# Products of 512 columns from both parts of the activation, in place of two of 256

## The chip, the cores and the metric

The kernel runs on one core of one Trainium2 chip. The metric is the device time of one execution in microseconds; before the change it was 1375.06 us, the median of 3 runs (1374.87 to 1375.58).

## The reference, cut to what matters

The program is a block of three layers over 256 rows of 1024 numbers: a convolution mixer with a dense feed-forward network, an attention mixer with 8 experts, and a third layer with attention, a memory and a second dense feed-forward network. The change touches the convolution's input projection and both dense networks:

```python
b_gate, c_gate, u = jnp.split(h @ w_in, 3, axis=-1)     # h is 256 x 1024, w_in 1024 x 3072
v = c_gate * u                                          # then a causal convolution of width 3
...
x = x + (b_gate * conv) @ w_out
...
h = rmsnorm(x, norm_ffn[i])
x = x + (jax.nn.silu(h @ w_gate) * (h @ w_up)) @ w_down # w_gate, w_up 1024 x 2816
```

Everything is float32.

## The kernel before, in words

Float32 products are made of three faster ones. Each operand is split into a high part (rounded by ScalarE, `split_to`, L219) and a low part (the rest, subtracted by VectorE, L220); `mm3` adds up high x high, low x high and high x low (L225 to L227), all into one PSUM bank.

Weights come in chunks of 128 x 2048 (1 MB), loaded by SP into four raw buffers, and are split in two pieces of 128 x 1024 into three pairs of buffers. A chunk's load therefore waits until the chunk four places earlier is split, and a split waits until the products of the chunk three places earlier are done. `Body.run` walks through a list of steps and writes each engine's instructions in that order; `f` in an order string means one piece of a coming chunk. Every engine executes its own list in order.

The steps that matter:

- In the convolution, `x00` to `x11` (`features`) each use one chunk with two tiles of 128 weight columns. The weights are the still operand, the activation, turned so that its 1024 features lie in 8 blocks of 128 rows and the 256 positions in columns, is the moving one. Each tile gives one feature block of 128 x 256, in half a bank. `g0` to `g7` (`gated`) combine three such blocks and split the result; `o0`, `o1` and `zp` multiply it with the output weights. `C` loads constants, `T` makes the rope tables (`rope_tables`), which only the attention layer reads.
- In a feed-forward stage the first 512 columns of gate and up are made by rows (`a`, `A`), and turned by eight transposes on TensorE (`T`, `rows_turn`), whose two banks have the tag t. `u04` to `u21` (`up`) are made like the convolution's features: the gate half in one half of a bank, the up half in the other. `o` multiplies with the down weights and keeps four banks of tag b as sums.

PSUM has eight banks; six have the tag b, two the tag t. A bank is written again when all that reads its old contents is done.

Of the kernel before, what the change touches and what calls it, by code (L numbers as in the profile page):

```python
# [12 lines left out]
F32R = mybir.dt.float32r  # L13
# [3 lines left out]
AF = mybir.ActivationFunctionType  # L17
# [4 lines left out]
P = 128  # L22
D = 1024
S = 256
NT = S // P
KD = D // P
# [5 lines left out]
NH = 8  # L32
# [25 lines left out]
PIECES = 2  # L58
AHEAD = 2, 2

TAGS = dict(x8=2, n4=4, g4=1, c6=2, e1=6, q=4, w2=11, mk=1, vm=1, sel=2, mx=2, kr=1, ssr=1)
BANKS = dict(b=6, t=2)

WARM = 26
CONV_HEAD = ("zs00 zs01 zn0 zs10 zt f1 zs11 zn1 w")
CONV_ORDER = ("x00 x01 f1 f2 T x02 f2 x03 f2 f2 f2 C x04 f2 x05 g0 x06 g1 f2 f1 g2 x07 f1 f2 f1 f1 x08 o0 g3 f1 f2 "
    "f1 f1 g4 f2 x09 g5 x10 x11 f2 f1 o1 g6 g7 f2 zp000 f2 zp010 zp100 zp110 f2 zp001 zp011 f1 zr00 zp101 "
    "zr01 zp111 zs00 zs01 zn0 f1 f1 f2 zt zr10 f1 f2 f2 zs10 f1 zr11 f1 f1 zs11 zn1 f1")
FFN_HEAD = ("f1 f2 a00 f2 f1 a10 f2 f1 w a20 f1 f2 a21 a01 a30 f2 a31 f2 a11 f1 f2 f2 f2 f1 f1 f2 A u04 f2 f2 f2 "
    "f1 T f2 u05 f1 f1 f1 o0 o1 f2 f2 f2 f2 o2 f1 f2 f2 u06 f1 f2 u07 f1 f2 f1 f2 f1")  # L70
# [35 lines left out]
class Parts:  # L106


    def __init__(self, pieces):
        self.pieces = pieces  # L110

    def __call__(self, k, s=slice(0, S)):
        for k0, n, h, l in self.pieces:
# [4 lines left out]
class Body:  # L118
# [103 lines left out]
    def mm3(self, ps, a, b, start, stop):  # L222

        mm = self.nc.tensor.matmul
        mm(ps, lhsT=a[0], rhs=b[0], start=start, stop=False)  # L225
        mm(ps, lhsT=a[1], rhs=b[0], start=False, stop=False)  # L226
        mm(ps, lhsT=a[0], rhs=b[1], start=False, stop=stop)  # L227


    def row(self, name, n, tag=None):  # L230
# [153 lines left out]
    def conv(self, norm, nxt):  # L384
        nc, t_ = self.nc, self.t
        cin = [self.chunk(t_["conv_in"][i]) for i in range(12)]
        cout = [self.chunk(t_["conv_out"][i]) for i in range(4)]
        feat, got, acc = {}, {}, {}

        def features(i):  # L390
            c = cin[i]
            b = self.bank("b" if i % 3 != 1 else "t")
            for h in range(2):
                o = feat[2 * i + h] = b[:, h * S:(h + 1) * S]
                for k in range(KD):
                    w = slice((h * KD + k) * P, (h * KD + k + 1) * P)
                    self.mm3(o, c[w], norm.xT(k), k == 0, k == KD - 1)

        def gated(j):
            oc, ou, ob = (feat.pop(3 * j + i) for i in range(3))  # L400
            cw = self.cols[:, 0:24].rearrange("p (j w) -> p j w", w=3)
            cs, v, y, z = (self.buf("e1", [P, n]) for n in (S, S + 2, S, S))
            nc.scalar.copy(cs, oc)
            nc.gpsimd.memset(v[:, :2], 0.0)
            nc.vector.tensor_mul(v[:, 2:], cs, ou)
            nc.vector.tensor_scalar(y, v[:, :S], cw[:, j, 0:1], None, op0=ALU.mult)
            for q in (1, 2):
                nc.vector.scalar_tensor_tensor(y, v[:, q:q + S], cw[:, j, q:q + 1], y, op0=ALU.mult, op1=ALU.add)
            nc.vector.tensor_mul(z, y, ob)
            got[j] = self.split(z)  # L410

        def out(d):
            for r in range(2):
                self.project(acc, cout[d], r, got.pop(2 * d + r), d == 0 and r == 0)

        closing = self.closing(acc, [(cout[j // 2], j % 2, lambda j=j: got[j]) for j in range(4, 8)], nxt, False)
        self.play(CONV_HEAD, self.entering(norm))
        self.play(CONV_ORDER, {
            "x": lambda i, j: (lambda: features(10 * i + j), cin[10 * i + j]), "g": lambda j: (lambda: gated(j),),
            "o": lambda d: (lambda: out(d), cout[d]), "C": lambda: (self.constants,), "T": lambda: (self.rope_tables,), **closing})  # L420


    def ffn(self, norm, gu0, gu, down, nxt, orders):

        nc = self.nc
        c0 = [self.chunk(gu0[i]) for i in range(4)]
        cu = [self.chunk(gu[i]) for i in range(NF - 4)]
        cd = [self.chunk(down[i]) for i in range(NF // 2)]
        acc, got, rows = {}, {}, {}

        def row_part(i, t):

            if i % 2 == 0:
                rows[i // 2, t] = self.bank()
            for kk in range(4):
                k = 4 * (i % 2) + kk
                self.mm3(rows[i // 2, t], norm.xT(k, slice(t * P, (t + 1) * P)), c0[i][kk * 512:(kk + 1) * 512],
                         k == 0, k == KD - 1)

        def rows_act():  # L440
            hs = []
            for t in range(NT):
                sg, h = self.buf("w2", [P, 512]), self.buf("w2", [P, 512])
                nc.scalar.activation(sg, rows[0, t], AF.Silu)
                nc.vector.tensor_mul(h, sg, rows[1, t])
                hs.append(h)
            rows["h"] = hs

        def rows_turn():
            th, tl = self.buf("n4", [P, 4, S], F32R), self.buf("n4", [P, 4, S], F32R)  # L450
            for t in range(NT):
                b = self.bank("t")
                for k in range(4):
                    nc.tensor.transpose(b[:, k * P:(k + 1) * P], rows["h"][t][:, k * P:(k + 1) * P], self.ident)
                ts = slice(t * P, (t + 1) * P)
                self.split_to(th[:, :, ts], tl[:, :, ts], b.rearrange("p (k m) -> p k m", m=P))
            for k in range(4):
                got[k] = th[:, k], tl[:, k]

        def up(j):  # L460
            b = self.bank()
            for i in range(2):
                for k in range(KD):
                    w = slice((i * KD + k) * P, (i * KD + k + 1) * P)
                    self.mm3(b[:, i * S:(i + 1) * S], cu[j - 4][w], norm.xT(k), k == 0, k == KD - 1)
            sg, h = self.buf("e1", [P, S]), self.buf("e1", [P, S])
            nc.scalar.activation(sg, b[:, :S], AF.Silu)  # L467
            nc.vector.tensor_mul(h, sg, b[:, S:])  # L468
            got[j] = self.split(h)

        def out(d):
            for r in range(2):
                self.project(acc, cd[d], r, got.pop(2 * d + r), d == 0 and r == 0)

        d = NF // 2 - 2
        step = self.closing(acc, [(cd[j // 2], j % 2, lambda j=j: got[j]) for j in range(2 * d, NF)], nxt, False)
        step.update({
            "a": lambda i, t: (lambda: row_part(i, t), c0[i]), "w": lambda: (lambda: norm.turn(1),),
            "A": lambda: (rows_act,), "T": lambda: (rows_turn,),
            "u": lambda i, j: (lambda: up(10 * i + j), cu[10 * i + j - 4]), "o": lambda d: (lambda: out(d), cd[d])})  # L480
        self.play(orders[0], step)
        for j in range(8, NF):
            self.add(lambda j=j: up(j), cu[j - 4])
            if j % 2 == 1 and j < NF - 1:
                d = (j - 3) // 2
                self.add(lambda d=d: out(d), cd[d])
        self.play(orders[1], step)
# [75 lines left out]
    def mla(self, norm, nxt, other):  # L563
# [109 lines left out]
        def values(c):  # L673
            d = st.pop(c)
            if c == 0:
                g["oh"], g["ol"] = self.buf("x8", [P, NH, S], F32R), self.buf("x8", [P, NH, S], F32R)
            o = self.bank("t")
            for h in range(2):
                self.causal_values(o[:, h * S:(h + 1) * S], d["v"][:, :, h], d["pT", h])
            hs = slice(2 * c, 2 * c + 2)  # L680
            self.split_to(g["oh"][:, hs], g["ol"][:, hs], o.rearrange("p (h s) -> p h s", s=S))
# [452 lines left out]
class Norm:  # L1134
# [33 lines left out]
    def turn(self, t):  # L1168
        b, nc = self.b, self.b.nc
        if t == 0:  # L1170
            if self.whole:
                h, l = b.buf("x8", [P, KD, S], F32R), b.buf("x8", [P, KD, S], F32R)
                self.pieces = [(k0, n, h[:, k0:k0 + n], l[:, k0:k0 + n]) for k0, n, _ in self.cut]
            else:
                self.pieces = [(k0, n, b.buf(tag, [P, n, S], F32R), b.buf(tag, [P, n, S], F32R))
                               for k0, n, tag in self.cut]
            self.xT = Parts(self.pieces)
        for k0, n, h, l in self.pieces:
            b.transposed(self.h[t][:, k0 * P:(k0 + n) * P], n, h, l, t)

# [21 lines left out]
class Experts:  # L1202
# [84 lines left out]
    def plan(self, nxt, other):  # L1287
# [3 lines left out]
        def work(e, i, ns=(0, 1)):  # L1291

            c = self.chunks[24 * e + i]
            if i == 0:
                s["th"], s["tl"] = (b.buf("x8", [P, FE // P, CAP], F32R) for _ in range(2))
                if e % 2 == 0:
                    s["pair"] = self.next
                s["a"] = s["pair"].of(e % 2)
# [57 lines left out]
    def slow(self):  # L1356

        b, nc = self.b, self.b.nc
        for e in range(NE):
# [9 lines left out]
            for j in range(2):  # L1369
                self.gather(sel, j)  # L1370
            back = self.back(sel, 0)
            th, tl = (b.buf("x8", [P, FE // P, CAP], F32R) for _ in range(2))
            for half in range(2):
                g, u = self.two(), self.two()
                product(g, 8 * half, sel.of(0), KD)
# [145 lines left out]
```

## Time and profile before

| | |
|---|---|
| median of 3 runs | 1375.06 us |
| profiled execution | 1372.2 us, its span 1370.5 us |
| TensorE (PE) busy | 1318.7 us, 96%, 7267 matmuls |
| VectorE (DVE) busy | 1014.6 us, 74% |
| ScalarE (ACT) busy | 816.9 us, 60% |
| DMA | 329.53 MB, 240 GB/s on average |
| mean granted TensorE clock | 0.99 |

The convolution runs from 15.5 to 109 us, the first feed-forward stage to about 300, the second from about 1176 to the end. Matmuls are pipelined: one of 256 columns is shown 283 ns long, but the next one starts earlier than that. How fast TensorE goes is read from starts, not from lengths. "Idle before" is the time in which an engine did nothing, with what ended it.

### The profile page before, as it was taken

The numbers are of one execution on the slowest core, as the hardware profiler recorded it, in microseconds if no ns is written. First come the engines' busy times: TensorE is split into PE (matmuls) and PEld (weight loads), VectorE is DVE, ScalarE is ACT, GpSimd is POOL, SyncE is SP. The second block draws the span as 40 slices with busy tenths as digits, with TensorE's granted clock in tenths as the row PEclk, the third lists the DMA queues.
The fourth block names the chain that finished last, engine by engine and source line by source line (L and its number), as shares of the span: only waits on it lengthen the run. The fifth ranks groups of instructions, "written<-read, shape, count | busy, mean of one in ns | idle before, by whom it ended". The sixth has DMA issues, their size and how long they took to land.

```text
span 1370.5 us, 18683 instructions
## 1 busy us (share of the span) xinstructions
PE 1318.7 (96%) x7267; PEld 1134.3 (83%) x7267; DVE 1014.6 (74%) x1348; ACT 816.9 (60%) x1200; POOL 35.3 (3%) x70
## 2 busy tenths in 40 slices
PE   7999999999996999999999999999989888999998
PEld 7997999988775888888888888888868777899997
DVE  5876465567767999899999999999976666654554
ACT  4545354446754877777777777777754555543442
POOL 1000000001100000000000000000002000000000
PEclk9999999999998999999999999999999999999999
DMA  7545555536333899999999999999963332544551
GB/s 276 218 169 188 181 200 185 187 101 193 122 140 128 342 369 352 332 365 369 361 340 344 356 358 354 345 357 369 361 230 133 138 114 88 184 155 184 185 185 62
DMA packets 49328, 329.53 MB, mean 240 GB/s; under 512 B 6352, under 2 KB 7248, under 8 KB 11216
## 3 DMA queue, kind: packets, MB, share of 16 engines
q1 hardware_dynamic: 48672, 328.18, 65.1%
q8 instruction: 58, 0.95, 0.3%
q14 instruction: 38, 0.31, 0.1%
q10 hardware_dynamic: 560, 0.09, 0.0%
HBM read 327.20 MB, written 1.05 MB: 240 GB/s over the span
## 4 chain that ended last, share of the span: by engine, by line
PE 63%; DVE 3%; ACT 1%; issue 0%; POOL 0%; DVEq 0%; ACTq 0%; POOLq 0%
PE ps L225 19%; PE ps L227 19%; PE ps L226 19%; DVE wl L220 1%; PE ps L1267 1%; PE ps L1230 1%; PE ps L1277 0%; PE ps L1276 0%; ACT wh L219 0%; DVE e L899 0%; PE ps L710 0%; PE ps L559 0%; DVE n L1166 0%; PE ps L508 0%; PE ps L1038 0%
## 5 line engine op out<-in xcount | busy, mean ns | idle before, releaser
L220 DVE TENSOR_TENSOR wl<-raw,wh 128x1024 fp32r<-128x1024 f32 (+2 forms) x622 | 716.7, 1201 | 101.0 <-ACT wh L219 98.8
L219 ACT CAST wh<-raw 128x1024 fp32r<-128x1024 f32 (+2 forms) x622 | 611.2, 1034 | 130.6 <-PE ps L226 91.7
L225 PE MATMUL ps<-x,wh 128*128 128x256 f32 x800 | 227.3, 284 | 0.7 <-DVE c L220 0.5
L226 PE MATMUL ps<-x,wl 128*128 128x256 f32 x800 | 226.7, 283 | 0.3 <-DVE wl L220 0.3
L227 PE MATMUL ps<-x,wh 128*128 128x256 f32 x800 | 226.8, 283 | 0.0
L225 PE MATMUL ps<-wh,n 128*128 128x512 f32 x560 | 220.8, 394 | 0.0
L227 PE MATMUL ps<-wl,n 128*128 128x512 f32 x560 | 218.5, 390 | 0.0
L226 PE MATMUL ps<-wh,n 128*128 128x512 f32 x560 | 218.0, 389 | 0.0
L225 PE MATMUL ps<-wh,x 128*128 128x512 f32 (+2 forms) x448 | 175.6, 392 | 0.3 <-ACT x L219 0.2
L227 PE MATMUL ps<-wl,x 128*128 128x512 f32 (+2 forms) x448 | 173.3, 387 | 1.4 <-DVE wl L220 1.4
L226 PE MATMUL ps<-wh,x 128*128 128x512 f32 (+2 forms) x448 | 172.7, 386 | 1.1 <-DVE x L220 1.1
L225 PEld LDWEIGHTS ps<-x,wh 128*128 128x128 f32 x800 | 153.8, 192 | 2.3 <-DVE c L220 0.8
L226 PEld LDWEIGHTS ps<-x,wl 128*128 128x128 f32 x800 | 153.8, 192 | 1.3 <-DVE wl L220 0.5
L227 PEld LDWEIGHTS ps<-x,wh 128*128 128x128 f32 x800 | 153.8, 192 | 0.2 <-DVE x L220 0.2
L227 PEld LDWEIGHTS ps<-wl,n 128*128 128x128 f32 x560 | 105.1, 188 | 22.9
L226 PEld LDWEIGHTS ps<-wh,n 128*128 128x128 f32 x560 | 105.2, 188 | 21.4
L225 PEld LDWEIGHTS ps<-wh,n 128*128 128x128 f32 x560 | 105.2, 188 | 21.2
L227 PEld LDWEIGHTS ps<-wl,x 128*128 128x128 f32 x448 | 84.1, 188 | 20.0 <-DVE wl L220 3.2
L467 ACT ACTIVATE e<-ps 128x256 f32<-128x256 f32 x36 | 13.9, 385 | 144.8 <-PE ps L227 144.8
L226 PEld LDWEIGHTS ps<-wh,x 128*128 128x128 f32 x448 | 84.2, 188 | 17.3 <-DVE x L220 2.1
L225 PEld LDWEIGHTS ps<-wh,x 128*128 128x128 f32 x448 | 84.2, 188 | 15.7 <-ACT x L219 0.7
L468 DVE TENSOR_TENSOR e<-e,ps 128x256 f32<-128x256 f32 x36 | 15.2, 421 | 101.2 <-ACT e L467 101.2
(301 smaller groups left out, 1412.9 us busy)
## 6 DMA issues: line engine op xcount, KB each, us to landing
raw<-in_moe SPq DMA_DIRECT2D x192, 1024.0 KB, 5.5
raw<-in_ffn_gu SPq DMA_DIRECT2D x22, 1024.0 KB, 4.9
raw<-in_gu SPq DMA_DIRECT2D x22, 1024.0 KB, 4.9
raw<-in_conv_in SPq DMA_DIRECT2D x11, 1024.0 KB, 6.5
raw<-in_ffn_down SPq DMA_DIRECT2D x11, 1024.0 KB, 5.0
raw<-in_down SPq DMA_DIRECT2D x11, 1024.0 KB, 5.2
raw<-in_w_mem SPq DMA_DIRECT2D x6, 1024.0 KB, 4.9
raw<-in_w_in SPq DMA_DIRECT2D x6, 1024.0 KB, 4.9
```

The lines of the kernel that those rows point to most:

```text
L219: self.nc.scalar.copy(hi, src)
L220: self.nc.vector.tensor_tensor(lo, src, hi.bitcast(F32), ALU.subtract)
L225: mm(ps, lhsT=a[0], rhs=b[0], start=start, stop=False)
L226: mm(ps, lhsT=a[1], rhs=b[0], start=False, stop=False)
L227: mm(ps, lhsT=a[0], rhs=b[1], start=False, stop=stop)
L467: nc.scalar.activation(sg, b[:, :S], AF.Silu)
L468: nc.vector.tensor_mul(h, sg, b[:, S:])
L1230: nc.tensor.matmul(ps[:, q * w:(q + 1) * w], lhsT=rows, rhs=sel.rearrange("p i m -> p (i m)"), start=i == 0, stop=i == len(todo) - 1)
L1267: nc.tensor.transpose(ps[:, k * P:(k + 1) * P], h[n][:, k * P:(k + 1) * P], b.ident)
```

## The change

The two parts of the turned activation now lie side by side in one tile, 128 x 8 x 2 x 256. For each of the 8 blocks `wide` makes one product of the high weights with 512 columns (high part in the bank's first half, low part in its second) and one of the low weights with 256 columns, into the first half. Each feature has a bank to itself, and `halves` adds the two halves: ScalarE copies one, VectorE adds the other. Which banks they are follows from parity: in a feed-forward stage both of an odd step's banks have the tag t, both of an even step's the tag b. The tiles of tag x8 are halved in number and doubled in size, also where attention and experts use them. The order string of the convolution is a new one: `C` stands before x02, `T` behind x05, and the gated steps begin earlier.

```diff
-TAGS = dict(x8=2, n4=4, g4=1, c6=2, e1=6, q=4, w2=11, mk=1, vm=1, sel=2, mx=2, kr=1, ssr=1)
+TAGS = dict(x8=1, n4=4, g4=1, c6=2, e1=6, q=4, w2=11, mk=1, vm=1, sel=2, mx=2, kr=1, ssr=1)
...
-CONV_ORDER = ("x00 x01 f1 f2 T x02 f2 x03 f2 f2 f2 C x04 f2 x05 g0 x06 g1 f2 f1 g2 x07 f1 f2 f1 f1 x08 o0 g3 f1 f2 "
+CONV_ORDER = ("x00 x01 f1 f2 C x02 f2 x03 f2 g0 f2 x04 f2 g1 f2 x05 g2 f2 T x06 g3 f1 f2 x07 f1 g4 f2 x08 f1 f1 o0 g5 "
...
+    def wide(self, ps, w, xT):
+
+
+        mm = self.nc.tensor.matmul
+        for k in range(KD):
+            x = xT.both[:, k].rearrange("p c s -> p (c s)")
+            h, l = w(k)
+            if k < KD - 1:
+                mm(ps, lhsT=h, rhs=x, start=k == 0, stop=False)
+            mm(ps[:, :S], lhsT=l, rhs=x[:, :S], start=False, stop=False)
+            if k == KD - 1:
+                mm(ps, lhsT=h, rhs=x, start=False, stop=True)
+
+    def halves(self, ps):
+
+        o = self.buf("e1", [P, S])
+        self.nc.scalar.copy(o, ps[:, S:])
+        self.nc.vector.tensor_add(o, o, ps[:, :S])
+        return o
...
-            b = self.bank("b" if i % 3 != 1 else "t")
             for h in range(2):
-                o = feat[2 * i + h] = b[:, h * S:(h + 1) * S]
-                for k in range(KD):
-                    w = slice((h * KD + k) * P, (h * KD + k + 1) * P)
-                    self.mm3(o, c[w], norm.xT(k), k == 0, k == KD - 1)
+                o = feat[2 * i + h] = self.bank("t" if h and (i % 2 or i > 8) else "b")
+                self.wide(o, lambda k: c[(h * KD + k) * P:(h * KD + k + 1) * P], norm.xT)
...
-            cs, v, y, z = (self.buf("e1", [P, n]) for n in (S, S + 2, S, S))
-            nc.scalar.copy(cs, oc)
+            cs, us = self.halves(oc), self.halves(ou)
+            v, y, z = (self.buf("e1", [P, n]) for n in (S + 2, S, S))
             nc.gpsimd.memset(v[:, :2], 0.0)
-            nc.vector.tensor_mul(v[:, 2:], cs, ou)
+            nc.vector.tensor_mul(v[:, 2:], cs, us)
...
-            nc.vector.tensor_mul(z, y, ob)
+            nc.vector.tensor_mul(z, y, self.halves(ob))
...
-            b = self.bank()
+            b = [self.bank("t" if j % 2 else "b") for _ in range(2)]
             for i in range(2):
-                for k in range(KD):
-                    w = slice((i * KD + k) * P, (i * KD + k + 1) * P)
-                    self.mm3(b[:, i * S:(i + 1) * S], cu[j - 4][w], norm.xT(k), k == 0, k == KD - 1)
+                self.wide(b[i], lambda k: cu[j - 4][(i * KD + k) * P:(i * KD + k + 1) * P], norm.xT)
             sg, h = self.buf("e1", [P, S]), self.buf("e1", [P, S])
-            nc.scalar.activation(sg, b[:, :S], AF.Silu)
-            nc.vector.tensor_mul(h, sg, b[:, S:])
+            nc.scalar.activation(sg, self.halves(b[0]), AF.Silu)
+            nc.vector.tensor_mul(h, sg, self.halves(b[1]))
             got[j] = self.split(h)
...
-                h, l = b.buf("x8", [P, KD, S], F32R), b.buf("x8", [P, KD, S], F32R)
+                both = b.buf("x8", [P, KD, 2, S], F32R)
+                h, l = both[:, :, 0], both[:, :, 1]
```

On VectorE the start of the rope tables (`posf`, then the use of `rowinv_freq`) stood in the convolution between the first and second piece of x03's weights (`wl_301`); before the change:

```order
L220 TENSOR_TENSOR wl_295<-raw_116,wh_294 128x1024 x2
L220 TENSOR_TENSOR wl_301<-raw_118,wh_300 128x1024
L303 CAST posf<-pos 128x2
L310 TENSOR_SCALAR w_27_314<-rowinv_freq_310,posf 128x32 x2
L313 TENSOR_SCALAR w_28_317<-w_27_314 128x64
L314 CAST w_29_318<-w_28_317 128x64
L315 CAST w_28_317<-w_29_318 128x64
L317 SCALAR_TENSOR_TENSOR w_27_314<-w_28_317,w_27_314 128x64 x3
```

With the change it stands behind g2's last instruction and x07's weights (`wl_531`), and the next gated step and x08's weights follow it:

```order
L221 TENSOR_TENSOR w_56_527<-e_54_517,w_56_527 128x256
L221 TENSOR_TENSOR wl_531<-raw_343,wh_530 128x1024 x2
L324 CAST posf<-pos 128x2
L331 TENSOR_SCALAR w_58_546<-rowinv_freq_542,posf 128x32 x2
L334 TENSOR_SCALAR w_59_549<-w_58_546 128x64
L335 CAST w_60_550<-w_59_549 128x64
L336 CAST w_59_549<-w_60_550 128x64
```

The block moved behind the rest of x03's pieces, those of x04 to x07, and three gated steps. On SP the row of frequencies was loaded behind the chunk of x06 (`raw_304`); before:

```order
L194 DMA raw_243<-in_conv_in 128x2048
L194 DMA raw_304<-in_conv_in 128x2048
L234 DMA rowinv_freq_310<-in_rows 128x32
L194 DMA raw_397<-in_conv_in 128x2048
L194 DMA raw_454<-in_conv_in 128x2048
```

With the change it is loaded behind the chunk of x10 (`raw_536`):

```order
L195 DMA raw_452<-in_conv_in 128x2048
L195 DMA raw_536<-in_conv_in 128x2048
L255 DMA rowinv_freq_542<-in_rows 128x32
L195 DMA raw_635<-in_conv_in 128x2048
L195 DMA raw_698<-in_conv_out 128x2048
```

In both, the chunk ahead of it takes the raw buffer of the chunk whose pieces stand on VectorE just ahead of the tables (x02's before, x07's after). On TensorE the end of u04 in the first feed-forward stage is followed by the transposes and u05; before, with the waits of each:

```order
L454 MATMUL ps_1458<-ident,w_113_1385 128x128 [waits DVE_49,PE_49]
L454 MATMUL ps_1458<-ident,w_113_1385 128x128 x3
L454 MATMUL ps_1465<-ident,w_115_1389 128x128 [waits DVE_49,PE_49]
L454 MATMUL ps_1465<-ident,w_115_1389 128x128 x3
L225 MATMUL ps_1472<-x_94_1204,wh_1374 128x256 [waits Activation_49]
L226 MATMUL ps_1472<-x_94_1204,wl_1375 128x256
```

With the change (`ps_1323` and `ps_1330` are the transposes' banks, `ps_1337` is u05's first):

```order
L472 MATMUL ps_1323<-ident,w_139_1259 128x128 [waits DVE_49,PE_49]
L472 MATMUL ps_1323<-ident,w_139_1259 128x128 x3
L472 MATMUL ps_1330<-ident,w_141_1263 128x128 [waits DVE_49,PE_49]
L472 MATMUL ps_1330<-ident,w_141_1263 128x128 x3
L238 MATMUL ps_1337<-x_121_1079,wh_1248 128x512 [waits DVE_49]
L239 MATMUL ps_1337<-x_121_1079,wl_1249 128x256
```

The order of the steps is the same; what u05's first product waits for was ScalarE and is now VectorE. The second feed-forward stage reads alike.

## Rows read from the trace of the kernel before

**Rows 1.** Windows of 25 us: busy us (count) of PE, PEld, DVE, ACT, POOL; clock; DMA.

```profile
50.00:75.00 25.00, 25.00 (x188) 23.91 (x187) 19.59 (x30) 11.61 (x16) 0.30 (x3) 1.00 0.52 191
...
175.00:200.00 25.00, 25.00 (x189) 23.91 (x187) 15.01 (x18) 13.45 (x19) 0.00 (x0) 1.00 0.70 253
```

**Rows 2.** Timeline of PE: start, length, line, tiles, shape.

```profile
134.58 0.28 PE L225 MATMUL ps<-x,wh 128*128 128x256 f32 x1
...
140.33 1.04 PE L454 MATMUL ps<-ident,w 128*128 128x128 f32 x8
...
141.12 0.36 PE L225 MATMUL ps<-x,wh 128*128 128x256 f32 x1
...
146.96 0.40 PE L225 MATMUL ps<-wh,n 128*128 128x512 f32 x1
...
157.86 0.40 PE L225 MATMUL ps<-wh,w 128*128 128x512 f32 x1
...
163.46 0.28 PE L225 MATMUL ps<-x,wh 128*128 128x256 f32 x1
...
1205.51 0.36 PE L225 MATMUL ps<-x,wh 128*128 128x256 f32 x1
```

**Rows 3.** Timeline of ACT and DVE, both feed-forward stages, around the transposes.

```profile
140.53 0.38 ACT L467 ACTIVATE e<-ps 128x256 f32<-128x256 f32 x1 [4.29 <-PE ps L227]
...
145.07 1.28 DVE L220 TENSOR_TENSOR n<-ps,n 128x512 fp32r<-128x512 f32 x2
...
1209.46 1.28 DVE L220 TENSOR_TENSOR n<-ps,n 128x512 fp32r<-128x512 f32 x2
```

**Rows 4.** Timeline of DVE in the convolution: gated steps and weights.

```profile
45.05 0.41 DVE L405 TENSOR_TENSOR e<-e,ps 128x256 f32<-128x256 f32 x1
...
48.23 0.41 DVE L405 TENSOR_TENSOR e<-e,ps 128x256 f32<-128x256 f32 x1
...
52.02 3.50 DVE L220 TENSOR_TENSOR wl<-raw,wh 128x1024 fp32r<-128x1024 f32 x3 [0.53 <-ACT wh L219]
```

**Rows 5.** Timeline of SP and DVE around the rope tables; one row of DMA landings.

```profile
23.11 0.33 SPq L194 DMA_DIRECT2D raw<-in_conv_in  x1
...
23.48 0.77 SPq L234 DMA_DIRECT2D rowinv_freq<-in_rows  x1
...
30.50 0.39 DVE L310 TENSOR_SCALAR w<-rowinv_freq,posf 128x32 f32<-128x32 f32 x2
...
35.45 0.19 DVE L336 TENSOR_SCALAR sin<-sin 128x64 f32<-128x64 f32 x1
...
cols<-in_cols ACTq DMA_DIRECT2D x1, 20.0 KB, 1.7
```

**Rows 6.** Timeline of DVE and PE in the convolution.

```profile
15.51 0.69 DVE L220 TENSOR_TENSOR x<-ps,x 128x512 fp32r<-128x512 f32 x1 [1.19 <-ACT x L219]
...
37.56 0.39 PE L226 MATMUL ps<-x,wl 128*128 128x256 f32 x1 [0.31 <-DVE wl L220]
...
69.22 0.40 PE L225 MATMUL ps<-wh,w 128*128 128x512 f32 x1
```

**Rows 7.** Groups by form: busy us, mean ns of one, idle before.

```profile
L220 DVE TENSOR_TENSOR wl<-raw,wh 128x1024 fp32r<-128x1024 f32 x596 | 698.4, 1220 | 100.5 <-ACT wh L219 98.3
...
L219 ACT CAST wh<-raw 128x1024 fp32r<-128x1024 f32 x596 | 594.9, 1049 | 127.2 <-PE ps L226 90.8 <-issue 25.1 <-PE ps L227 3.0
```

**Rows 8.** Windows behind idle time of PE; the column before the DMA share is the clock.

```profile
1017.40:1021.30 3.90, 0.38 (x2) 0.00 (x0) 2.33 (x5) 2.99 (x6) 0.56 (x1) 1.00 0.50 162
...
1021.40:1024.80 3.40, 3.23 (x12) 2.94 (x13) 2.63 (x7) 1.78 (x4) 0.56 (x1) 0.50 0.27 111
...
1085.20:1087.00 1.80, 0.24 (x3) 0.05 (x1) 1.80 (x7) 0.37 (x1) 0.00 (x0) 1.00 0.91 264
...
1087.00:1090.40 3.40, 2.79 (x20) 2.47 (x21) 1.89 (x7) 2.29 (x10) 0.00 (x0) 1.00 0.42 173
```

More of the change, by code (lines that the diff above doesn't have):

```diff
@@ L65 @@
 CONV_HEAD = ("zs00 zs01 zn0 zs10 zt f1 zs11 zn1 w")
-CONV_ORDER = ("x00 x01 f1 f2 T x02 f2 x03 f2 f2 f2 C x04 f2 x05 g0 x06 g1 f2 f1 g2 x07 f1 f2 f1 f1 x08 o0 g3 f1 f2 "
-    "f1 f1 g4 f2 x09 g5 x10 x11 f2 f1 o1 g6 g7 f2 zp000 f2 zp010 zp100 zp110 f2 zp001 zp011 f1 zr00 zp101 "
+CONV_ORDER = ("x00 x01 f1 f2 C x02 f2 x03 f2 g0 f2 x04 f2 g1 f2 x05 g2 f2 T x06 g3 f1 f2 x07 f1 g4 f2 x08 f1 f1 o0 g5 "
+    "f2 f1 x09 f2 f1 x10 g6 f2 x11 f2 f1 o1 g7 f2 zp000 f2 zp010 zp100 zp110 f2 zp001 zp011 f1 zr00 zp101 "
     "zr01 zp111 zs00 zs01 zn0 f1 f1 f2 zt zr10 f1 f2 f2 zs10 f1 zr11 f1 f1 zs11 zn1 f1")
@@ L106, with __init__ @@
 class Parts:
-    def __init__(self, pieces):
+    def __init__(self, pieces, both=None):
         self.pieces = pieces
+        self.both = both
     def __call__(self, k, s=slice(0, S)):
@@ L675, in values @@
             if c == 0:
-                g["oh"], g["ol"] = self.buf("x8", [P, NH, S], F32R), self.buf("x8", [P, NH, S], F32R)
+                o = self.buf("x8", [P, 2, NH, S], F32R)
+                g["oh"], g["ol"] = o[:, 0], o[:, 1]
             o = self.bank("t")
@@ L1176, in turn @@
                                for k0, n, tag in self.cut]
-            self.xT = Parts(self.pieces)
+            self.xT = Parts(self.pieces, both if self.whole else None)
         for k0, n, h, l in self.pieces:
@@ L1294, in work @@
             if i == 0:
-                s["th"], s["tl"] = (b.buf("x8", [P, FE // P, CAP], F32R) for _ in range(2))
+                both = b.buf("x8", [P, 2, FE // P, CAP], F32R)
+                s["th"], s["tl"] = both[:, 0], both[:, 1]
                 if e % 2 == 0:
@@ L1371, in slow @@
             back = self.back(sel, 0)
-            th, tl = (b.buf("x8", [P, FE // P, CAP], F32R) for _ in range(2))
+            both = b.buf("x8", [P, 2, FE // P, CAP], F32R)
+            th, tl = both[:, 0], both[:, 1]
             for half in range(2):
```

## The prediction, made before the changed kernel ran

> **What bounds the kernel now.** I read the page first: TensorE is busy for 96% of the span, VectorE for 74%, ScalarE for 60%. The table by windows of 25 us then shows where. In the convolution and in the first feed-forward stage TensorE is busy for 25.00 of 25 us, VectorE for 19.59 and 15.01 [rows 1]. So in the stages that the change touches, TensorE's own pace sets the time, and VectorE is nearer to its limit in the convolution. Busy time hides the pace, since matmuls overlap, so I took it from starts in the timeline. From 134.58 to the transposes at 140.33 stand 48 products of 256 columns, 119.8 ns each; from 146.96 to 157.86 stand 48 products of 512 columns, 227.1 ns each; the next 24, whose still operand is another tile, take 233.3 ns each to 163.46 [rows 2].
>
> **What the change removes.** Per 128 rows of the contraction, three products of 256 columns (359.4 ns) become one of 512 and one of 256 (346.9 ns): 12.5 ns saved. There are 24 features in the convolution and 36 in each feed-forward stage, with 8 such steps each: 768 steps, 9.6 us. A step with the slower wide product (233.3 ns) saves 6.3 ns, 4.8 us in all. I take 12.5, because most 512-column products run at that pace; both ends stay in the range. One chunk of weights (16 steps) takes 5.55 us in place of 5.75.
>
> The Trainium skill ("TensorE: Matmul & The Clock Gate", Back-to-back issue gap) gives an isolated warm product N/2.4 + 2.5 ns, that is 109 and 216 ns here. The trace disagrees: 119.8 and 227.1. By the page the saving would be only 2.5 ns a step, 1.9 us in all.
>
> **What it adds.** Each finished feature costs a ScalarE copy of 128x256 and a VectorE sum. The nearest rows are 0.38 us for ScalarE's read of a bank [rows 3] and 0.41 for VectorE's with a bank as operand [rows 4]. A gated step had one copy already, so it gains two copies and three sums. In the trace it takes VectorE 3.18 us (45.05 to 48.23) [rows 4]; three sums make it 4.4. An up step gains two of each; with one step to about 5.6 us of TensorE these fit into idle time of both engines, except in two places.
>
> **Place one: the rope tables (T) in the convolution.** They move from before x02 to after x05, behind the second piece of x07's weights on VectorE, and ahead of the third gated step and of x08's weights. VectorE executes in order, so everything behind T waits with it. T needs a row of inverse frequencies, which SP loads behind a weight chunk that itself waits until VectorE has finished a chunk. In the trace SP issues the chunk at 23.11, the row at 23.48, and the first instruction that uses it starts at 30.50 [rows 5]. So T begins 7.4 us after the chunk's issue, and lasts from 30.50 to 35.45 + 0.19 = 35.64, 5.1 us. Before, this idle time lay under a lead; now it doesn't, as this sum shows.
>
> TensorE: x08 ended and o0 began at 69.22 [rows 6], nine chunks of 5.75 us, which puts an even start at 17.5. I take 0.5 off for a wait on x03's weights behind T, which goes (the product at 37.56), and add 0.3 since the first wide product needs the low half of the activation too, which is ready at 15.51 + 0.69 = 16.20 [rows 6]. So 17.3; x02 ends at 17.3 + 3 x 5.55 = 33.95, and x07 at 61.7.
>
> VectorE: the weights have three buffers, so x05's can't be split before x02 ends. From 33.95: cast 1.05 and subtraction 1.22 [rows 7] give 36.2; g0 4.4, 40.6; three pieces with their hand-over 0.53 + 3.50 [rows 4], 44.65; g1 and g2, 53.45; x07's two pieces 0.53 + 2.34, 56.3; wait for the row 7.4, 63.7; T 5.1, 68.8; g3 4.4, 73.2; x08's first piece 0.53 + 1.17, 74.9. TensorE wants it at 61.7, so it stands 13.2 us. Against before, x08 starts at 74.9 instead of 69.22 - 5.75 = 63.5: 11.4 late. After that x08 to x11 give back 4 x 0.20 = 0.8. VectorE then has some 40 us of work (eight chunks of 2.34 and their hand-overs, four gated steps) under 44 us of TensorE's: tight, and I count nothing there, up to 3 at the upper end.
>
> The unknown in it is how soon the row lands. The nearest small load took 1.7 us [rows 5]; then T would begin 5.2 earlier and the stall would be 8. I take 7.4, since the order of issue is the same as in the row. The constants (C) move earlier, into a time of heavy loads; ScalarE then waits for the load between 1.7 us and the row's 7.0 (23.48 to 30.50), which adds 0 to 1.5 to the sum.
>
> **Place two: u05 behind the transposes, in both feed-forward stages.** The eight transposes of T (here rows_turn) fill both banks of tag t. Before, u05 wrote a bank of tag b and started at once: 141.12, after the transposes at 140.33 [rows 2]. Now j = 5 is odd, so u05 takes the same two banks, and TensorE waits until VectorE has split them. Those splits start at 145.07 and take 1.28 for two, so the first bank is free at 145.7 [rows 3]. Ahead of them, u04's end gets one more operation in the chain: a copy and a sum take the place of the activation and multiplication that followed the last product, and the multiplication comes after (0.41 and a hand-over, 0.5). So 146.2 against 141.12: 5.1 us. In the second such stage 1209.46 + 0.64 + 0.5 = 1210.6 against 1205.5, again 5.1 [rows 2, 3].
>
> **The clock.** After 3.90 us with 0.38 of work the next 3.40 us were granted 0.50, the 1.2 GHz level; after 1.80 us with 0.24 of work the next stayed at 1.00 [rows 8]. All three stalls are longer than the first of these. Such a stretch costs up to 1.7 us if work lies in it and nothing if it falls into the stall. I take 1.7 for the long stall and 0.9 for each of 5.1; the ends are 0 and 3.4, and 0 and 1.7.
>
> The activation's halves now lie side by side, so their writes are strided. No row shows it; the writes keep their 128x512 size, and I take 0, with half a microsecond to either side.
>
> **The sum.** Convolution: 11.4 - 0.8 + 1.7 = +12.3. Each feed-forward stage: 18 chunks x 0.20 = 3.6 saved, 5.1 + 0.9 lost, +2.4. Together +17.1 on the span of 1370.5, or 1387.6. The profiled execution took 1372.2, 2.9 under the median of 1375.06; adding 17.1 to the median gives 1392.
>
> **Rivals.**
> *Neither wait binds.* Then only the shorter steps count: 1375.06 - 9.6 = 1365.5, faster. For it speaks that TensorE is the busiest engine throughout and VectorE idles for 5 to 10 us in 25 [rows 1]. Against it, both waits follow from orders that each engine keeps. It decides if x08's weights are split by 61.7, 13 us sooner than my chain gives.
> *Only the feed-forward waits.* The row lands early and VectorE's chain gains on TensorE: -9.6 + 10.2 + 1.8 = +2.4, 1377.5. For it: small loads do land in 1.7 us [rows 5]. Against: T's work and g3 alone, with no wait at all for the row, still put x08 at 67.5, after 61.7.
> *Only the convolution's wait.* u05's banks come free in time: +12.3 - 7.2 = +5.1, 1380. Against: the splits began 4.7 us behind the transposes in both stages [rows 2, 3].
> *The wide product is slow.* At 233.3 ns or more, and if VectorE falls behind once more in the convolution: half of the gain goes, 0.4 + 3.6, some 1396; with 3 more behind x08, 1399. For it: products with one kind of still operand do run so [rows 2]. The page of the skill above would go a little further, to some 1399 without the 3.
>
> **How the numbers follow.** My sum 0.73; neither wait 0.06; only feed-forward 0.07; only convolution 0.05; slow 0.09. The likeliest gives 1392 with its own range of 1384 to 1399 (quick landing and no clock loss; slow product and late constants). To leave out no more than two in ten I go from 1379 to 1402. What this measurement can tell from no change is 0.2%, 2.75 us: faster under 1372.3, slower over 1377.8. Faster 0.06 (neither wait), same 0.08 (most of the case with feed-forward alone, and near misses), slower 0.86.
>
> **What would show it.** In the profile after: products of 512 columns on the wide line about 227 ns apart, and 768 fewer matmuls; one idle stretch of TensorE near 61 us, about 13 us long, ended by VectorE's subtraction of weights, and under it VectorE idle for some 5 to 7 us until the row lands, then T; two idle stretches of about 5 us after the eight transposes, ended by VectorE's split of the transposed rows; a lower granted clock behind each. The forecast is wrong if T's first instruction follows x07's weights without a wait, if u05 follows the transposes within 1 us, or if the steps are much under 340 ns.

## The result: slower, 1397.3 us

The changed kernel takes 1397.32 us (median of 4 runs, 1396.75 to 1397.86) against 1375.32 for the kernel before beside it: 22.0 us more, ratio 1.0156 [1.0144, 1.0169]. The forecast was 1392, its range 1379 to 1402.

The first line of the page after, and the new VectorE group (its columns: busy us, mean ns of one, idle time before it):

```profile
PE 1327.0 (95%) x6499; PEld 1103.8 (79%) x6499; DVE 1051.8 (75%) x1444; ACT 844.9 (61%) x1288; POOL 35.2 (3%) x70
...
L247 DVE TENSOR_TENSOR e<-e,ps 128x256 f32<-128x256 f32 x96 | 39.4, 417 | 87.9 <-ACT e L246 87.9
```

There are 768 matmuls fewer than the 7267 of before, and TensorE is busy 8 us longer all the same. A sum of two halves takes VectorE 417 ns, as the 0.41 us of [rows 4] had it. The stages have to be compared by their borders. The first transposes behind the convolution, behind the first feed-forward stage, and ahead of the second one, in the timeline of TensorE after:

```profile
122.87 1.29 PE L727 MATMUL ps<-ident,n 128*128 128x128 f32 x8 [0.62 <-DVE n L1183]
...
317.46 0.27 PE L727 MATMUL ps<-ident,n 128*128 128x128 f32 x1
...
1202.58 0.27 PE L727 MATMUL ps<-ident,n 128*128 128x128 f32 x1
```

And before:

```profile
109.59 0.33 PE L710 MATMUL ps<-ident,n 128*128 128x128 f32 x1 [0.54 <-DVE n L1166]
...
300.30 0.27 PE L710 MATMUL ps<-ident,n 128*128 128x128 f32 x1
...
1181.76 0.38 PE L710 MATMUL ps<-ident,n 128*128 128x128 f32 x2
```

With the spans (1395.5 and 1370.5) the differences give: convolution +13.3 us, first feed-forward stage 194.6 against 190.7 (+3.9), second 192.9 against 188.7 (+4.2), and the stages between, which the change hardly touches, 885.1 against 881.5 (+3.7). The three changed stages make 21.4, close to the 22.0 of the medians. The 3.7 between need not come from the change: the profiled execution of before was itself 2.9 us under its median, and in experiment ten, which has no part of the change, the stages between are 4.2 us longer than in that execution.

**The convolution.** VectorE's timeline (the brackets hold the idle time before a row and what ended it) and SP's, around the rope tables; in the places of [rows 5]:

```profile
56.03 2.36 DVE L221 TENSOR_TENSOR wl<-raw,wh 128x1024 fp32r<-128x1024 f32 x2 [0.53 <-ACT wh L220]
...
63.51 0.39 DVE L331 TENSOR_SCALAR w<-rowinv_freq,posf 128x32 f32<-128x32 f32 x2 [5.04 <-DMA rowinv_freq<-in_rows]
...
68.45 0.19 DVE L357 TENSOR_SCALAR sin<-sin 128x64 f32<-128x64 f32 x1
...
73.52 3.49 DVE L221 TENSOR_TENSOR wl<-raw,wh 128x1024 fp32r<-128x1024 f32 x3 [0.52 <-ACT wh L220]
...
58.80 0.42 SPq L255 DMA_DIRECT2D rowinv_freq<-in_rows  x1
```

TensorE at the same time:

```profile
64.03 0.39 PE L241 MATMUL ps<-x,wh 128*128 128x512 f32 x1
...
73.54 0.80 PE L238 MATMUL ps<-x,wh 128*128 128x512 f32 x1 [9.11 <-ACT wh L220]
...
74.80 0.58 PE L239 MATMUL ps<-x,wl 128*128 128x256 f32 x1 [0.46 <-DVE wl L221]
```

x07 ends at 64.3. VectorE has split x07's weights by 58.4 and waits 5.04 us for the row of frequencies, which SP issued only at 58.80. The tables and g3 follow, to 73.0; ScalarE's part of x08's weights stands behind g3 too. TensorE's first product waits 9.11 us for that, and the second 0.46 more for VectorE's part. The trace has no other wait of TensorE there: what holds x08 back is the order of VectorE and ScalarE behind one small load, which experiments one and two put to the test.

**The feed-forward stages.** TensorE at u05 and VectorE's split of the transposed rows, in the places of [rows 2, 3]:

```profile
153.42 1.03 PE L472 MATMUL ps<-ident,w 128*128 128x128 f32 x8
...
159.39 0.79 PE L238 MATMUL ps<-x,wh 128*128 128x512 f32 x1 [4.93 <-DVE n L221]
...
158.65 1.28 DVE L221 TENSOR_TENSOR n<-ps,n 128x512 fp32r<-128x512 f32 x2
...
1225.41 1.04 PE L472 MATMUL ps<-ident,w 128*128 128x128 f32 x8
...
1231.33 0.79 PE L238 MATMUL ps<-x,wh 128*128 128x512 f32 x1 [4.88 <-DVE n L221]
```

u05 started 0.79 us behind the transposes before; now it starts 5.97 and 5.92 behind, and VectorE's `n`, the read of the transposes' banks, lets it go.

**The clock.** Windows over the stretches of lower granted clock at the start and at these waits (columns as in [rows 1]):

```profile
12.10:22.30 10.20, 7.86 (x26) 6.62 (x27) 7.88 (x11) 5.90 (x7) 3.17 (x11) 0.50 0.87 348
...
66.70:80.30 13.60, 6.30 (x19) 5.03 (x19) 11.51 (x28) 5.26 (x12) 0.20 (x2) 0.50 0.22 78
...
158.80:162.30 3.50, 2.91 (x9) 2.53 (x10) 1.13 (x2) 0.00 (x0) 0.00 (x0) 0.51 0.65 239
...
1230.60:1237.50 6.90, 6.17 (x19) 5.31 (x20) 1.51 (x4) 0.37 (x1) 0.00 (x0) 0.51 0.42 154
```

And at the start of the kernel before:

```profile
11.10:17.90 6.80, 4.13 (x17) 3.71 (x18) 4.49 (x8) 2.94 (x6) 3.21 (x12) 0.50 1.00 416
```

The 0.50 (the 1.2 GHz level) at x08 begins within the wait and lasts to 80.3, so that 6.8 us of it have work in them: 3.4 us lost. At the start it lasts to 22.3, where before it ended at 17.9.

**The pace.** Four features without a wait, from the first wide product to the first product behind them:

```profile
211.03 0.40 PE L238 MATMUL ps<-x,wh 128*128 128x512 f32 x1
...
211.26 0.27 PE L239 MATMUL ps<-x,wl 128*128 128x256 f32 x1
...
211.38 0.40 PE L238 MATMUL ps<-x,wh 128*128 128x512 f32 x1
...
222.23 0.40 PE L226 MATMUL ps<-wh,w 128*128 128x512 f32 x1
```

32 steps in 11.20 us, 350 ns each, against 359.4 from [rows 2]. A wide product is followed after 0.23 us, a narrow one after 0.12.

### The profile page after: what moved, and what is told of

Read it like the earlier page. It is cut to its first block, busy times and chain, and to the rows that moved or that the text cites. A ratio compares the mean times of both kernels' runs of the same rounds, so it can differ in the third digit from the quotient of the medians.

```text
span 1395.5 us, 17386 instructions
## 1 busy us (share of the span) xinstructions
PE 1327.0 (95%) x6499; PEld 1103.8 (79%) x6499; DVE 1051.8 (75%) x1444; ACT 844.9 (61%) x1288; POOL 35.2 (3%) x70
## 4 chain that ended last, share of the span: by engine, by line
PE 62%; DVE 4%; ACT 1%; issue 0%; POOL 0%; DVEq 0%; ACTq 0%; POOLq 0%
PE ps L226 17%; PE ps L228 16%; PE ps L227 16%; PE ps L238 4%; PE ps L239 2%; DVE wl L221 1%; PE ps L1285 1%; PE ps L1248 1%; PE ps L241 1%; PE ps L1294 0%; PE ps L1295 0%; PE ps L524 0%; PE ps L575 0%; ACT wh L220 0%; DVE e L916 0%
## 5 line engine op out<-in xcount | busy, mean ns | idle before, releaser
L238 PE MATMUL ps<-x,wh 128*128 128x512 f32 x672 | 248.6, 407 | 19.5 <-DVE n L221 9.8
L239 PE MATMUL ps<-x,wl 128*128 128x256 f32 x768 | 203.7, 286 | 0.5 <-DVE wl L221 0.5
L238 PEld LDWEIGHTS ps<-x,wh 128*128 128x128 f32 x672 | 130.6, 194 | 48.5 <-DVE n L221 10.3
L239 PEld LDWEIGHTS ps<-x,wl 128*128 128x128 f32 x768 | 149.4, 195 | 9.9 <-DVE wl L221 1.0
L247 DVE TENSOR_TENSOR e<-e,ps 128x256 f32<-128x256 f32 x96 | 39.4, 417 | 87.9 <-ACT e L246 87.9
L246 ACT COPY e<-ps 128x256 f32<-128x256 f32 x96 | 33.8, 366 | 90.5 <-PE ps L241 90.5
L220 ACT CAST x<-ps 128x512 fp32r<-128x512 f32 x64 | 36.7, 588 | 54.7 <-PE ps L1285 32.2
L226 PE MATMUL ps<-wh,w 128*128 128x512 f32 x176 | 69.4, 395 | 0.0
```

Source lines behind the costliest of these rows:

```text
L220: self.nc.scalar.copy(hi, src)
L238: mm(ps, lhsT=h, rhs=x, start=k == 0, stop=False)
L239: mm(ps[:, :S], lhsT=l, rhs=x[:, :S], start=False, stop=False)
L246: self.nc.scalar.copy(o, ps[:, S:])
L247: self.nc.vector.tensor_add(o, o, ps[:, :S])
```

## The experiments

**One: the rope loads early.**

```diff
+        pos = c.tile([P, NT], I32, name="pos")      # now with the constants, C
+        nc.scalar.dma_start(pos, ...)
+        self.rope_in = pos, self.row("inv_freq", 32)
...
+        pos, fr = self.rope_in                      # in rope_tables, T
...
-        fr = self.row("inv_freq", 32)
```

> The two loads of the rope tables (positions, frequencies) are issued with the constants, ahead of x02; the tables' arithmetic stays behind x05 on VectorE. Theory (the order on VectorE makes TensorE stand before x08, first for the landing of the frequencies, then for the arithmetic): VectorE's 5.0 us of idle time ahead of the tables go, x08's weights come 5 us earlier, TensorE's idle time of 10.3 us falls to about 5, and the time from 1397.3 to about 1392 (1390 to 1393). Rival (VectorE is overloaded in the convolution anyway, and the landing lies beside it): x08 starts as late as before, 1396 to 1398.

Measured: 1390.42 us, ratio to before 1.0107 [1.009, 1.0124]; 6.9 less than the changed kernel. TensorE and VectorE, where x08 waited:

```profile
58.08 0.39 DVE L332 TENSOR_SCALAR w<-rowinv_freq,posf 128x32 f32<-128x32 f32 x2
...
68.12 0.79 PE L238 MATMUL ps<-x,wh 128*128 128x512 f32 x1 [4.12 <-ACT wh L220]
...
69.38 0.58 PE L239 MATMUL ps<-x,wl 128*128 128x256 f32 x1 [0.47 <-DVE wl L221]
```

VectorE no longer waits ahead of the tables, and TensorE's wait falls from 9.11 to 4.12 us. So 5 us of the long wait were the row's landing; the rest is VectorE's own work, as experiment two shows.

**Two: the tables' arithmetic out of the convolution too.**

```diff
-"... x04 f2 g1 f2 x05 g2 f2 T x06 g3 ..."
+"... x04 f2 g1 f2 x05 g2 f2 x06 g3 ..."
...
-"... u06 f1 f2 u07 f1 f2 f1 f2 f1"
+"... u06 f1 f2 u07 f1 f2 f1 f2 f1 R"                # R: rope_tables; the loads early as in one
```

> As the run with early loads, and the tables' arithmetic is moved out of the convolution, behind u07 of the first feed-forward stage. Theory: x08's weights are split at about 64.4 us, where x07 ends at 64.3, so nothing of the 10.3 us of idle time stays, nor the half clock behind it: x08 ends near 70 in place of 82.8, 12.9 us less, 1384.4 (1383 to 1386). Rival (VectorE's sums and gated steps alone are too much for the convolution): a stall of 3 to 5 us stays before x08 or comes before x09, 1387 to 1390.

Measured: 1386.74 us, 1.0078 [1.0061, 1.0095]. x08 now follows x07 at pace (64.08 and 64.31 in TensorE's timeline; the last row is the first transposes behind the convolution):

```profile
64.08 0.40 PE L241 MATMUL ps<-x,wh 128*128 128x512 f32 x1
...
64.31 0.40 PE L238 MATMUL ps<-x,wh 128*128 128x512 f32 x1
...
110.42 1.29 PE L728 MATMUL ps<-ident,n 128*128 128x128 f32 x8 [0.63 <-DVE n L1184]
```

The convolution ends at 110.42 in place of 122.87, that is 12.45 earlier, about the whole of its loss. The time is 2.3 us above what was expected, for the first feed-forward stage is 2.5 us longer than in the changed kernel. The tables make a new wait there (the product behind that of 194.23 starts 0.70 us late), and the stage is 1.4 us longer than in experiment one. The other 1.1 is in experiment one too: in both, the stretch at 0.50 behind u05's wait lasts 6.8 us, in the changed kernel 3.4, although the wait is the same 4.93 us.

**Three: u05 away from the transposes' banks.**

```diff
-            b = [self.bank("t" if j % 2 else "b") for _ in range(2)]
+            b = [self.bank("t" if j % 2 and j > 5 else "b") for _ in range(2)]
```

> u05 takes two banks of tag b in place of the transposes' banks, in both feed-forward stages; nothing else. Theory: u05 starts at once behind the transposes, two stalls of 5.2 us go, and with them the half clock behind each (some 1.4 us of loss each): 1397.3 - 13.2 = 1384 (1382.5 to 1386). Rival (the wait only moves: the first down product needs the same splits and comes next in the first stage): the first stage's gain is lost and the sum is 1390 to 1391.

Measured: 1380.35 us, 1.0037 [1.0023, 1.0051], 17.0 less than the changed kernel. Transposes and u05 in both stages:

```profile
151.25 1.03 PE L472 MATMUL ps<-ident,w 128*128 128x128 f32 x8
...
152.04 0.48 PE L238 MATMUL ps<-x,wh 128*128 128x512 f32 x1
...
1215.80 1.03 PE L472 MATMUL ps<-ident,w 128*128 128x128 f32 x8
...
1216.59 0.48 PE L238 MATMUL ps<-x,wh 128*128 128x512 f32 x1
```

u05 follows after 0.79 us again. The first stage is 188.1 us long (194.6 with the wait), the second 185.1 (192.9): the two waits cost 14.3, with the clock behind them. The other 3.2 of the span lie elsewhere, 2.1 of them in the convolution, where the stretches at 0.50 were shorter in this execution; they are no gain of the edit, and with them the time is under the expected range. Even so this edit of one number is worth more than both edits of the convolution: 14.3 against the 12.45 that the convolution gained, 17.0 against 10.6 by the medians.

**Four: both edits.**

> Both repairs: tables' loads early and their arithmetic in the first feed-forward stage, and u05 in banks of tag b. Theory: the gains add up, 1397.3 - 12.9 - 13.2 = 1371.2 (1369 to 1373.5), under the kernel before (1375.3), since 768 steps take some 351 ns in place of 360. Rival (the added copies and sums cost more than the products save): 1375 to 1378.

Measured: 1370.88 us, 0.9966 [0.9952, 0.998]: faster than before. The two mechanisms account for the whole loss. The gain left is 0.34%, 4.6 us, not 9.6. In the changed stages one new wait is left, behind the tables in their new place:

```profile
187.21 0.50 PE L228 MATMUL ps<-wl,w 128*128 128x512 f32 x1 [0.53 <-DVE wl L221]
```

**Five: wide products grouped** (five to eight build on experiment four, called the base).

```diff
...
+            for k in range(KD - 1):
+                mm(ps, lhsT=w(k)[0], rhs=x[k], start=k == 0, stop=False)      # 7 wide
             for k in range(KD):
...
+                mm(ps[:, :S], lhsT=w(k)[1], rhs=x[k][:, :S], ...)             # 8 narrow
+            mm(ps, lhsT=w(KD - 1)[0], rhs=x[KD - 1], start=False, stop=True)
```

> The kernel with both waits removed (1370.9 us, the base), and in each feature the seven wide products of 512 columns first, then the eight of 256, then the last wide one: the same products in another order. In the base a wide product is followed after 233 ns, a narrow one after 118, 351 a step. My theory: the 233 comes from the change of shape behind it (48 wide products in a row stood 227.1 ns apart in the kernel before); then a step falls to about 347 ns, 768 steps x 4.5 ns = 3.4 us less, some 1367.5. Rival: 233 is the pace of a wide product whose moving operand is this tile, whatever follows it; then 1371 and 233 ns between wide products in a row.

Measured: 1369.35 us, 0.9955 [0.9942, 0.9969]; the interval overlaps that of experiment four. One feature, and the product behind four of them:

```profile
208.36 1.76 PE L236 MATMUL ps<-x,wh 128*128 128x512 f32 x7
...
209.96 1.12 PE L238 MATMUL ps<-x,wl 128*128 128x256 f32 x8
...
210.91 0.40 PE L239 MATMUL ps<-x,wh 128*128 128x512 f32 x1
...
219.53 0.39 PE L226 MATMUL ps<-wh,w 128*128 128x512 f32 x1
```

And four features of the base:

```profile
209.76 0.39 PE L238 MATMUL ps<-x,wh 128*128 128x512 f32 x1
...
221.00 0.39 PE L226 MATMUL ps<-wh,w 128*128 128x512 f32 x1
```

Seven wide products take 1.60 us, 229 ns each; the narrow ones behind them 119. Four features take 11.17 us, 349 ns a step: 2 ns below the base's 351 (11.24 us), not 4; in the second feed-forward stage, where the base takes 350, it is 1 ns. Neither theory held whole: a wide product behind another takes less than 233 but not 227.1, and a narrow one behind a wide one gains some 2 ns that grouping gives back.

**Six: the merge undone in six of eight steps.**

```diff
-                mm(ps, lhsT=h, rhs=x, start=k == 0, stop=False)
+                if k == 0:
+                    mm(ps, lhsT=h, rhs=x, start=True, stop=False)
+                else:
+                    mm(ps[:, :S], lhsT=h, rhs=x[:, :S], start=False, stop=False)
+                    mm(ps[:, S:], lhsT=h, rhs=x[:, S:], start=False, stop=False)
```

> The base (both waits removed, 1370.9 us), with the merge undone in six of the eight steps of each feature: three products of 256 columns into the same two halves of the bank, so banks, copies, sums and the order of the steps stay. 48 features... (24 + 36 + 36 = 96 features) x 6 = 576 steps. My theory: a step goes from 351 ns to the 359.4 of the kernel before, 576 x 8.4 ns = +4.8 us, some 1375.7, and the matmuls rise by 576. By my prediction's terms (12.5 ns a step) +7.2, 1378. Rival, the estimate from the page of the Trainium skill (TensorE: Matmul & The Clock Gate, Back-to-back issue gap): 2.5 ns a step, +1.4, 1372.3, which would mean that the merge is worth nothing that can be measured.

Measured: 1373.71 us, 0.9987 [0.9978, 0.9996]; 2.8 more than the base, with 7075 matmuls. Four features:

```profile
210.25 0.39 PE L239 MATMUL ps<-x,wh 128*128 128x512 f32 x1
...
221.63 0.39 PE L226 MATMUL ps<-wh,w 128*128 128x512 f32 x1
```

11.38 us, 0.14 more than the base's 11.24; in the second feed-forward stage it is 0.19 (11.39 against 11.20). There are 24 such groups in the kernel, so 3.4 to 4.6 us by the traces and 2.8 by the medians, between the 4.8 of the theory and the 1.4 of the rival. The gain of the merge is real, and small.

**Seven: TensorE kept busy at the start.**

```diff
-CONV_HEAD = ("zs00 zs01 zn0 zs10 zt f1 zs11 zn1 w")
+CONV_HEAD = ("zs00 zs01 zn0 zs10 zt Y f1 zs11 zn1 w")
...
+            for i in range(38):                                               # Y
+                nc.tensor.transpose(b[:, i % 4 * P:(i % 4 + 1) * P], self.ident, self.ident)
```

> The base (both waits removed, 1370.9 us), with 38 transposes of the identity into a bank that nobody reads, put between the first eight transposes and the second eight at the start, where TensorE is idle for about 5 us. Theory of the clock: the idle time at the start is what brings the stretch at 0.50 from 11.3 to 21.5 us, in which the first products of the convolution (16.3 to 21.5) go at half pace; with the idle time filled they go at 1.00 and 2.6 us are saved, some 1368.3. Rival: the stretch comes from what lies before 8 us and stays; then 1371, or up to 2 more where the added transposes themselves delay the second eight.

Measured: 1369.08 us, 0.9955 [0.9941, 0.9968], 1.8 less than the base; the intervals overlap, but the profile is plain. The stretch from 11.3 to 21.5 in this kernel, with the row that fills it:

```profile
9.27 4.31 PE L439 MATMUL ps<-ident 128*128 128x128 f32 x38
...
11.30:21.50 10.20, 8.92 (x60) 7.59 (x59) 8.50 (x11) 6.23 (x9) 3.17 (x11) 1.00 0.90 357
```

and in the base:

```profile
9.30:13.80 4.50, 0.01 (x1) 0.04 (x1) 3.64 (x7) 2.03 (x4) 1.42 (x5) 0.72 1.02 429
...
11.30:21.50 10.20, 7.16 (x24) 6.08 (x25) 7.88 (x11) 5.93 (x8) 3.16 (x11) 0.50 0.87 345
```

The granted clock is 1.00 in place of 0.50, and the convolution ends 2.0 us earlier (107.91 against 109.88).

**Eight: all that helped.** Grouping, the filled start, and `R` moved ahead of u06, into idle time of VectorE.

> All that helped, together: both waits removed, wide products grouped, the idle time at the start filled, and the rope tables' arithmetic moved once more, from behind u07 to ahead of u06 in the first feed-forward stage, where VectorE was idle from 161.2 to 166.8 us and the tables last 5.2. My sum, from the base of 1370.9: grouping -1.5, the start -1.8 (as each measured alone), and -0.9 for the wait of 0.70 us behind the tables in the first feed-forward stage (186.28 us in the base, 6.5 us in place of 5.6 for its 24 products), some 1366.7. Rival: the differences of 1.5 and 1.8 are chance between runs, and the sum stays at 1369 to 1371. A wait of TensorE near 190 us that stays would speak against the third term.

Measured: 1366.62 us, 0.9929 [0.9916, 0.9943], as summed. TensorE has no wait near 190 us. This is the best of the kernels here, 9.3 us under the one before; the filled start, which has nothing to do with the merge, gave 1.8 of them in experiment seven (0.9 with the old products, in experiment ten).

**Nine: the layout alone, with the old products.**

```diff
...
-                h, l = b.buf("x8", [P, KD, S], F32R), b.buf("x8", [P, KD, S], F32R)
+                both = b.buf("x8", [P, KD, 2, S], F32R)
+                h, l = both[:, :, 0], both[:, :, 1]
...
```

> The kernel before with one part of the change alone: the two parts of the activation side by side in one tile, and the other tiles of tag x8 halved in number and doubled in size. Products, banks, sums and the order are the old ones. My prediction took nothing for it (half a microsecond to either side), so 1375.4. The stages between the two feed-forward stages are now 3.7 us longer than before in the changed kernel (885.1 against 881.5), 3.4 of it in the stage before the third layer's memory, where TensorE has a stretch at 0.50 of 13.65 us in place of 3.4. If the layout brings this, the time is some 1379 and the stretch from about 1079 us lasts 13.65; if it comes from where the stretch happens to begin, the layout leaves it at 3.4 or moves it with no other sign.

Measured: 1375.69 us, 1.0002 [0.9993, 1.0011]: the layout costs nothing.

**Ten: the kernel before with the filled start alone.**

> The kernel before, with the 38 transposes of the identity at the start alone, which took the stretch at 0.50 away in the changed kernel. In the kernel before the stretch lasts from 11.1 to 17.9 us and 2.4 us of the products lie in it, so 1.2 us are saved: 1374.2. By the theory of the clock a kernel that has no other edit, and only starts 1.2 us earlier, may also get another stretch in the memory stage (3.4 or 13.65 us, up to 5 us of time); the rival, that the old products always keep it at 3.4, expects 3.4 here.

Measured: 1374.86 us, 0.9991 [0.9982, 1.0], 0.9 of the 1.2 expected, at the edge of what can be told; in the traces the convolution ends 1.0 us earlier (108.59 against 109.59). Its memory stage:

```profile
1080.00:1093.70 13.70, 12.30 (x45) 9.88 (x46) 9.54 (x20) 7.66 (x18) 0.00 (x0) 0.50 0.22 78
```

and that of the profiled execution of before:

```profile
1079.40:1082.80 3.40, 3.13 (x13) 2.18 (x14) 2.28 (x5) 3.29 (x6) 0.00 (x0) 0.50 0.00 0
...
1082.80:1093.10 10.30, 7.95 (x57) 6.83 (x56) 8.20 (x18) 6.02 (x17) 0.00 (x0) 1.00 0.30 103
```

The old products, with no part of the change, have the long stretch too, as has experiment nine. Of the profiled kernels only the one before had the short one, in an execution of 1372.2 us with a mean granted clock of 0.990 (experiment six has 10.2 us there, all others 13.7). One of the 21 runs of before beside these two kernels took 1372.02, also at 0.990; the 20 others took 1374.6 or more, at 0.984 to 0.987. So the usual execution of before has more time at the lower clock than the profiled one; that it lies at this place fits, but isn't shown, since those runs have no trace.

## Why the prediction was right, point by point

- **Direction and places.** Right. Each wait lies where the chain put it, with the releaser named, and undoing both (four) turns the change into a gain.
- **The convolution, +12.3 forecast, +13.3 measured.** x08's second product starts at 74.80 where 74.9 was forecast, but that is luck: two errors cancel. VectorE reached the end of x07's weights at 58.4, not 56.3 (x02 had ended as much later, at 36.1), and the wait for the row was 5.04, not the 7.4 taken from [rows 5]. x07 ended at 64.3, not 61.7, since the first products ran at 0.50 until 22.3 and the steps were slower; so TensorE idled less than the 13.2 forecast, for the same end. The term that was too small is the clock behind the wait: 3.4 us lost, 1.7 forecast.
- **Each feed-forward stage, +2.4 forecast, +3.9 and +4.2 measured.** The wait was right at 5.1 (5.18 and 5.13 by starts). The clock was granted 0.50 for 2.9 us of work in the first and 6.2 in the second, so 1.4 and 3.1 lost where 0.9 was taken. With the convolution, the clock behind the three waits cost 7.9 where 3.5 was forecast, the largest error of the sum. Without the wait (three) the stages are 2.6 and 3.6 shorter than before; 288 steps of 9 ns make 2.6. The further 1.0 of the second is no gain of the products: the last store to `out` lands 3.37 us behind its issue in the three traces of the old products, with an 8 KB packet of instructions moved meanwhile, and 2.30 in the nine of the new ones, with none. That the packet is the cause isn't shown.
- **The step, 346.9 ns forecast, 350 measured.** This term was mis-sized too: 9 ns saved where I took 12.5, 7 us in all in place of 9.6. I had taken 227.1 ns, the pace of wide products behind one another with the normalized rows as still operand [rows 2]; with weights still and this tile moving it is 233, and 229 grouped. The row for it, 233.3 ns, stood in the same group, and I gave it to a rival. The gap that the Trainium skill ("TensorE: Matmul & The Clock Gate", Back-to-back issue gap) states for an isolated product gives, as an estimate, a saving of 2.5 ns a step. The traces disagree: 350 against 359.4 is 9, and experiment six undid 576 steps for 2.8 us by the medians and 3.4 to 4.6 by the traces, 5 to 8 ns each.
- **The layout, 0 forecast.** Right by experiment nine. The earlier constants, 0 to 1.5 forecast, cost TensorE nothing: ScalarE waits 4.70 us for their load, but TensorE has no idle time from 16.4 to the end of x07. **The rivals.** "Neither wait" falls with one and three, "only the convolution" with three; "only the feed-forward" falls with one and two. "The wide product is slow" was half right: its 233 ns came, the further delay of VectorE did not (x08 is at pace in two).
- **The base of the sum.** Adding to the median rather than to the profiled execution kept the sum good: the profiled execution of before is 2.9 us under its median.
- **What stays open.** Experiment four gains 4.6 us where, by the traces, the shorter steps and the quicker last store would give 8.3. The tables in the first feed-forward stage (189.6 us, against 188.1 in three) take 1.5 of that, more work at half clock at the start 1.4 (5.2 us at 0.50, against 2.4 before), and the later start of the first product 0.7 (16.28 against 15.53). Eight, which takes the first two away and groups, gains 9.3. Why a wait of 5 us is followed by 3.4 us at 0.50 in one place and by 6.8 in another stays open, and so does the reason for the quicker last store.

## What to carry to other kernels

A merge that saves 9 ns in 360, here 7 us, can be lost to one wait on a bank that two steps now share (6.5 and 7.8 us here, with the clock behind it); before counting such a gain, list who else has to leave each bank first, and what stands on the in-order engines ahead of the next operand. Take a pace from products with the same still and moving operands, since 6 ns decide here. Check that the profiled execution lies at the median, and has the mean granted clock of the other runs, before stages are subtracted.

## What the runs showed of the hardware

- Idle time of TensorE had a price beyond itself: behind the waits of 5 us the granted clock was 0.50 for 3.4 and 6.8 us (6.8 at both in experiments one and two), and at that of 10 us for 13.7 us, half of it within the wait. With the idle 5 us at the start filled, no such stretch came there (experiments seven, eight and ten).
- At one place (the memory stage, about 1079 us in the kernel before) kernels whose work there is the same got a stretch at 0.50 of 3.4, 10.2 or 13.7 us, and some 3 us of time go with the long one.
- A narrow product of 256 columns takes 117 ns behind a wide one and 119 behind its like; a wide one 233 or 229. The sum per step moved by 2 ns only.
